# Ordering the prologue loads, warming the matmul clock, and loading the exp table one stage earlier in a macaron FFN + chunked-attention block

## The chip, the cores and the metric

The kernel runs on the 8 cores of one Trainium2 chip. Each core takes one batch row of 4096 frames, all cores read the same weights, and there is no traffic between cores. The metric is the device time of the slowest core in microseconds (us), median of several executions.

In most executions all cores agree within half a per cent and the records show a mean granted TensorE clock of 0.991 to 0.998. In some executions the cores of one die (cores 0 to 3, or 4 to 7) show a lower clock, down to 0.81, and the time is some per cent longer, up to 3430 us.

## The reference

```python
def reference(x, norm_ffn1, ffn1_w_gate, ..., norm_final):      # cut: the list of weights
    x = x + 0.5 * swiglu(rmsnorm(x, norm_ffn1), ffn1_w_gate, ffn1_w_up, ffn1_w_down)
    h = rmsnorm(x, norm_mix)
    z = h @ w_in                                   # q, k, v (512 each), u and vs (512 each), 2 x 1024 gate logits
    y_att = chunked_rel_attention(q, k, v, rel_bias)     # own 64-frame chunk and 8 chunks to the left
    y_sgu = gelu(u) * spatial_mix(layernorm(gelu(vs)))   # gMLP gating on 128-frame blocks
    x = x + (sigmoid(g_att) * (y_att @ w_branch_att) + sigmoid(g_sgu) * (y_sgu @ w_branch_sgu)) @ w_out
    x = x + 0.5 * swiglu(rmsnorm(x, norm_ffn2), ffn2_w_gate, ffn2_w_up, ffn2_w_down)
    return rmsnorm(x, norm_final)
```

x is (8, 4096, 1024) in float32, the FFN width is 2816, and there are 8 heads of 64.

## The kernel before

The sequence is cut into 8 tiles of 512 frames. The Python program records operations for five engines, and each engine then executes its own list strictly in order, waiting on semaphores where the recorder found a dependency. So the place at which an operation is recorded decides what stands in front of it. The stages run in this order:

- FFN 1 of tile 0, the first four pieces of FFN 1 of tile 1 ("ahead"), and the input projection of tile 0;
- then for each tile t: attention(t) interleaved with FFN 1 of tile t+1, the merge and output projection of t, the input projection of t+1, and FFN 2 of t. Attention 7 is interleaved with FFN 2 of tile 6.

`interleave` spreads the 144 steps of an attention evenly over the 60 pieces of an FFN (44 gate and up pieces of 8 matmuls, 16 down pieces of 11):

```python
def interleave(main, side, n_main, n_side):
    done = 0
    for i in range(n_main):
        next(main, None)
        want = (i + 1) * n_side // n_main
        while done < want:
            next(side, None)
            done += 1
    # cut: drain both
```

Weights stream through six SBUF buffers (`SLOT`, 1 MiB of bf16 each). At first a weight chunk is float32 in HBM: a casting DMA, issued on GpSimd, reads 2 MiB and writes 1 MiB. At a chunk's first, second or third use (spread over the chunks by `convert_use`) SP writes it back to HBM as bf16, and later uses read that copy.

```python
            def pump():
                while nxt[0] < len(chunk_order) and (nxt[0] < NSLOT or rel_flag.get(nxt[0] - NSLOT)):
                    # cut: which chunk, which buffer
                    if chunk not in converted:
                        p.dma("pool", ..., reads=[("X", 0, 3, 0)] if k == 1 else [], writes=[("slot", i)], sem=f"slotq{i}")
                    else:
                        p.dma("sp", ..., reads=[("SCR", chunk)], writes=[("slot", i)], sem=f"slot{i}")
```

The beginning: x of tile 0 on two queues, all six slots at once (slot 1 and its followers in GpSimd's list wait for x), then four RMS norms. A norm squares on ScalarE with a row sum, takes the reciprocal root on GpSimd (`add`, then `pow` with -0.5), scales on VectorE or ScalarE, and transposes on TensorE.

```python
            load_x(0)
            if not dry:
                pump()
            # cut
            for s in range(4):
                norm_sq(0, 0, s)
                if s:
                    norm_cp(0, 0, s - 1, "dve")
                    norm_tr(0, 0, s - 1)
            norm_cp(0, 0, 3, "dve")
            norm_tr(0, 0, 3)
```

Hooks put other work between the pieces of an FFN. In the first FFN these are the loads of x of tile 1 (piece 10), of the constants (piece 16), and seven memsets and a multiply on VectorE (piece 40). In later ones the last final-norm multiply of two tiles before goes to piece 0, in front of the first attention steps:

```python
                if t == 0:
                    add_hook(hk, 16, const_loads)
                    add_hook(hk, 50, const_loads_late)
                    add_hook(hk, 40, const_ops)
                    # cut: if n_tiles > 1
                        add_hook(hk, 10, P(load_x, 1))
                # cut
                    if t >= 2:
                        add_hook(hk, 0, P(final_mul, t - 2, 3))
```

(Calls of the projection are put on shared lines here.) The gating layernorm (`sgu_ln`) of a tile is recorded on VectorE and GpSimd inside the projection, behind the copies of q; v is copied out of PSUM by VectorE:

```python
                def post_u(cc, b):
                    p.add("act", ... func=AF.Gelu_apprx_tanh ...)
                def post_v(s, b):
                    p.add("dve", lambda e: e.tensor_copy(out=VR[:, half * 4 + s, :], in_=bank(b)), ...)
                def post_q(cc, b):
                    # cut: two scaled copies on ScalarE
                    sgu_ln(cc)
                # cut
                win_rows(t, 4, post_vs); win_cols(t, 3, post_u); win_rows(t, 2, post_v)
                win_cols(t, 0, post_q);  win_cols(t, 1, post_k)
```

An attention step records the scores of item i, the normalisation of i-2, the transposes of i-3 and the product with v of i-4. Scores are summed with the bias and reduced on VectorE (`SC`, `ASTAT`), exponentiated on ScalarE (`PB`), transposed on TensorE and copied out of PSUM by ScalarE (`PTS`). There is one PSUM area for scores and one for transposes, so the scores of item i+1 wait until VectorE has read those of item i.

## Time and profile before

| | before |
|---|---|
| median of 3 runs | 2905.71 us (2902.48 to 2908.49) |
| span of the profiled execution, slowest core (6) | 2902.5 us |
| span, mean of 8 cores | 2897.5 us |
| mean granted clock, all cores | 0.994 to 0.996 |
| TensorE busy | 2799.8 us |

The page of the profile gives, for each engine, its busy time, share and instructions; then the span in 40 slices with the busy share in tenths:

```profile
PE 2799.8 (96%) x15372; PEld 1375.4 (47%) x15680; DVE 1262.0 (43%) x2468; ACT 1002.9 (35%) x1772; POOL 181.6 (6%) x420
...
PE   4999999999999999999999999999999999999998
```

TensorE (PE) is the bound. A full group of 8 matmuls starts every 1.73 us in this trace, and nothing in the change touches the number of matmuls of the model. Only the roughly 100 us in which TensorE is idle or slow can be won. The list of waits says where they are. Its columns are the waiting line, what it waited for, then us in total, number of waits, and the longest. L444 is a transpose of a norm, L482, L500 and L526 are the gate, up and down matmuls of an FFN, L683 and L687 are scores:

```profile
PE ps L444 <- DVE XN L431: 35.2, 4, 28.8
PE ps L683 <- DVE ASTAT L692: 14.6, 8, 2.1
PE ps L687 <- DVE ASTAT L692: 5.0, 1, 5.0
PE ps L526 <- DVE HT L509: 3.5, 2, 3.3
...
PE ps L482 <- DMA SLOT<-fsrc: 3.0, 1, 3.0
```

So: 35 us before the first matmuls; about 2.1 us at the start of each of attentions 1 to 6; 5.0 us in attention 0; 3.3 us behind the memsets at 125 us; 3.0 us for a weight slot.

The start, in order of time (columns: start, duration, engine and line, operation, output and input, shape and count, and in brackets the idle time before it and what ended it):

```profile
28.79 1.01 PE L444 MATMUL ps<-IDB,XN 128*128 128x128 bf16 x8 [28.79 <-DVE XN L431]
...
40.73 3.37 PE L482 MATMUL ps<-XT,SLOT 128*128 128x512 bf16 x8 [1.48 <-DVE XT L448]
43.94 1.89 PE L500 MATMUL ps<-XT,SLOT 128*128 128x512 bf16 x8
```

The first full group takes 3.37 us and later ones 1.89 us: the first runs at about half clock. (This is read from the durations; the clock records of this core begin at 43.8 us, with the full clock.)

The DMA engines are not idle meanwhile. This is their strip for the first 140 us on core 1, 40 slices of 3.5 us, busy share in tenths and GB/s written:

```profile
DMA  2999999999999999999999999999999999997100
GB/s 63 239 221 233 231 247 365 246 216 166 178 181 166 145 157 160 164 174 178 167 165 180 178 146 161 176 180 173 167 176 174 171 174 178 166 175 144 28 0 0
```

They are full from 3.5 us to about 126 us. A weight stream alone writes 160 to 180 GB/s, which means reading twice as much.

The start of attention 1, on all engines. The second scores are issued at 563.24 us (not shown), and the third have to wait:

```profile
561.13 1.28 DVE L827 SCALAR_TENSOR_TENSOR X<-X,STAT,GF 128x1024 f32<-128x1024 f32 x1
...
562.33 0.75 DVE L692 CUSTOM_DVE_ANT_0 SC<-ps,RB 128x576 f32<-128x576 f32 x1
...
563.17 1.28 ACT L699 ACT_TABLE_LOAD   x1 [2.81 <-DVE ASTAT L692]
...
564.46 0.78 ACT L699 ACTIVATE PB<-SC,ASTAT 128x576 bf16<-128x576 f32 x1
...
565.98 0.69 DVE L490 SCALAR_TENSOR_TENSOR TG<-TG,ps 128x512 f32<-128x512 f32 x1 [2.29 <-ACT TG L488]
...
567.49 0.32 PE L683 MATMUL ps<-KT,QBD 128*128 128x384 bf16 x1 [2.13 <-DVE ASTAT L692]
```

Read it backwards. The third scores wait for VectorE's reduction of the second (L692, at 566.59 us). That stands behind L490, which waited for ScalarE's tanh (L488), which stood behind the first exp (L699), which stood behind the load of the exp table: 1.28 us. The final-norm multiply (L827, 1.28 us) stands in front of the first reduction.

### The profile page before, as it was taken

Reading aid. Unit: us, or ns where it says so; the run is one execution under the profiler, and the core shown is the slowest. Engines: PE = TensorE matmul, PEld = TensorE weight load, DVE = VectorE, ACT = ScalarE, POOL = GpSimd, SP = SyncE. Lnnn points to the kernel's source line nnn. Section 1 sums busy time; section 2 is a strip of 40 time slices with the busy share of each in tenths; the row PEclk is TensorE's granted clock in tenths of the full one; section 3 lists DMA queues with packets and bytes.
Section 4 is the critical chain, followed back from the end, with each engine's and each line's share of the span. In section 5 each row is a group of like instructions: output and inputs, shape, how many; then the busy total and the mean of one; then the engine's idle time right before and its main releaser. Section 6 shows DMA issues by size and latency. Waiting matters only on the chain.

```text
span 2902.5 us, 44394 instructions; the slowest of 8 cores (2892.6 to 2902.5 us)
## 1 busy us (share of the span) xinstructions
PE 2799.8 (96%) x15372; PEld 1375.4 (47%) x15680; DVE 1262.0 (43%) x2468; ACT 1002.9 (35%) x1772; POOL 181.6 (6%) x420
## 2 busy tenths in 40 slices
PE   4999999999999999999999999999999999999998
PEld 2444444455444554445544454444544445445444
DVE  1336443364424644246442464425544255466332
ACT  1223332253322533224332343324433244345221
POOL 1110111100100000000000000000000000000000
PEclk9999999999999999999999999999999999999999
DMA  9899899997897434543444534445344452432352
GB/s 192 138 206 187 171 226 174 212 243 203 225 213 253 168 127 158 180 160 139 145 148 164 174 124 162 144 152 200 123 150 169 157 189 99 158 129 102 139 188 95
DMA packets 103434, 485.39 MB, mean 167 GB/s; under 512 B 8880, under 2 KB 9520, under 8 KB 85936
## 3 DMA queue, kind: packets, MB, share of 16 engines
q1 hardware_dynamic: 82288, 387.49, 38.4%
q0 software_dynamic: 20352, 93.92, 20.0%
q8 instruction: 131, 2.15, 0.3%
q10 hardware_dynamic: 576, 1.13, 0.1%
q14 instruction: 87, 0.71, 0.1%
HBM read 511.40 MB, written 65.01 MB: 199 GB/s over the span
## 4 chain that ended last, share of the span: by engine, by line
PE 85%; DVE 4%; DMA 4%; issue 4%; ACT 1%; POOL 1%; SPq 0%; DVEq 0%; ACTq 0%; POOLq 0%
PE ps L526 21%; PE ps L482 18%; PE ps L500 17%; PE ps L764 8%; PE ps L549 4%; PE ps L775 4%; PE ps L796 3%; PE ps L563 3%; PE ps L719 2%; DMA ffs<-SLOT 2%; PE ps L731 2%; PE ps L444 1%; DVE SC L692 1%; PE ps L687 1%; DMA wis<-SLOT 1%
## 5 line engine op out<-in xcount | busy, mean ns | idle before, releaser
L482 PE MATMUL ps<-XT,SLOT 128*128 128x512 bf16 x2718 | 664.4, 383 | 12.0 <-DMA SLOT<-fsrc 3.0
L500 PE MATMUL ps<-XT,SLOT 128*128 128x512 bf16 x2766 | 663.0, 380 | 2.7
L526 PE MATMUL ps<-SLOT,HT 128*128 128x512 bf16 x2738 | 623.6, 380 | 8.9 <-DVE HT L509 3.5
L509 DVE TENSOR_TENSOR HT<-ps,TG 128x512 bf16<-128x512 f32 x350 | 240.9, 689 | 431.4 <-PE ps L500 295.0
L482 PEld LDWEIGHTS ps<-XT,SLOT 128*128 128x128 bf16 x2816 | 270.4, 98 | 310.1 <-issue 16.2
L526 PEld LDWEIGHTS ps<-SLOT,HT 128*128 128x128 bf16 x2816 | 270.8, 98 | 307.1 <-issue 8.2
L500 PEld LDWEIGHTS ps<-XT,SLOT 128*128 128x128 bf16 x2816 | 269.5, 98 | 300.7 <-issue 4.7
L699 ACT ACTIVATE PB<-SC,ASTAT 128x576 bf16<-128x576 f32 (+7 forms) x256 | 190.7, 745 | 455.0 <-DVE ASTAT L707 358.2
L494 ACT ACTIVATE TG<-ps 128x512 f32<-128x512 f32 x178 | 106.1, 597 | 448.7 <-PE ps L482 423.3
L532 DVE SCALAR_TENSOR_TENSOR X<-ps,X 128x512 f32<-128x512 f32 x128 | 88.6, 692 | 383.3 <-PE ps L526 372.6
L764 PE MATMUL ps<-XT,SLOT 128*128 128x512 bf16 x999 | 238.1, 379 | 1.3
L490 DVE SCALAR_TENSOR_TENSOR TG<-TG,ps 128x512 f32<-128x512 f32 x174 | 119.7, 688 | 246.6 <-ACT TG L488 240.3
L692 DVE CUSTOM_DVE_ANT_0 SC<-ps,RB 128x576 f32<-128x576 f32 (+7 forms) x256 | 182.6, 713 | 43.7 <-PE ps L687 42.1
L722 ACT ACTIVATE PTS<-ps 128x640 bf16<-128x640 bf16 (+4 forms) x256 | 167.7, 655 | 39.7 <-PE ps L719 39.6
L549 PE MATMUL ps<-XT,SLOT 128*128 128x512 bf16 x751 | 167.5, 379 | 0.9
L769 ACT ACTIVATE TG<-ps,BG 128x512 f32<-128x512 f32 x128 | 87.9, 686 | 231.4 <-PE ps L764 231.4
L779 DVE SCALAR_TENSOR_TENSOR TG<-TG,ps 128x512 f32<-128x512 f32 x128 | 88.0, 688 | 175.5 <-PE ps L775 160.7
L448 DVE TENSOR_TENSOR XT<-ps,G 128x1024 bf16<-128x1024 bf16 x96 | 115.7, 1218 | 96.2 <-PE ps L444 96.2
L764 PEld LDWEIGHTS ps<-XT,SLOT 128*128 128x128 bf16 x1024 | 98.7, 98 | 112.3
L383 POOL TENSOR_SCALAR STAT<-STAT 128x1 f32<-128x1 f32 x128 | 24.5, 191 | 1923.9 <-ACT XN L417 1599.0
L417 ACT ACTIVATE XN<-X 128x1024 bf16<-128x1024 f32 x72 | 76.0, 1056 | 192.9 <-DVE X L801 80.2
L816 ACT ACTIVATE XN<-X 128x1024 bf16<-128x1024 f32 x32 | 33.8, 1057 | 251.3 <-DVE X L532 251.3
(78 smaller groups left out, 2363.2 us busy)
## 6 DMA issues: line engine op xcount, KB each, us to landing
SLOT<-ffs SPq DMA_DIRECT2D x128, 1024.0 KB, 5.8
SLOT<-fsrc POOLq DMA_DIRECT2D x48, 1024.0 KB, 17.7
SLOT<-wds SPq DMA_DIRECT2D x47, 1024.0 KB, 5.0
SLOT<-mgs SPq DMA_DIRECT2D x52, 768.0 KB, 5.4
SLOT<-wis SPq DMA_DIRECT2D x35, 1024.0 KB, 5.2
ffs<-SLOT SPq DMA_DIRECT2D x22, 1024.0 KB, 17.0
SLOT<-wds SPq DMA_DIRECT2D x23, 768.0 KB, 4.2
SLOT<-wd POOLq DMA_DIRECT2D x17, 1024.0 KB, 16.7
```

The lines of the kernel that those rows point to most:

```text
L448: p.add("dve", lambda e: e.tensor_tensor(out=XT[xt][:, :, s * 128:(s + 1) * 128], in0=pbf.rearrange("p (k c) -> p k c", k=8), in1=gb, op=A ...
L482: p.add("pe", lambda e, kc=kc, W=W, bg=bg: e.matmul(bank(bg), lhsT=W[:, kc * 128:(kc + 1) * 128], rhs=xt[:, kc, :], start=(kc == 0), stop= ...
L490: p.add("dve", lambda e, buf=buf, bg=bg: e.scalar_tensor_tensor(out=buf[:], in0=buf[:], scalar=1.0, in1=bank(bg), op0=ALU.add, op1=ALU.mul ...
L500: p.add("pe", lambda e, kc=kc, W=W, bu=bu: e.matmul(bank(bu), lhsT=W[:, 1024 + kc * 128:1024 + (kc + 1) * 128], rhs=xt[:, kc, :], start=(k ...
L509: p.add("dve", lambda e, buf=buf, bu=bu, fc=fc: e.tensor_tensor(out=HT[:, fc, :], in0=bank(bu), in1=buf[:], op=ALU.mult), reads=[rb(bu), b ...
L526: p.add("pe", lambda e, fc=fc, W=W, by=by, s=s: e.matmul(bank(by), lhsT=HT[:, fc, s * 128:(s + 1) * 128], rhs=W, start=(fc == 0), stop=(fc ...
L549: p.add("pe", lambda e, kc=kc, W=W, b=b, cc=cc: e.matmul(bank(b), lhsT=W[:, kc * 512 + cc * 128:kc * 512 + (cc + 1) * 128], rhs=XT[t % 2][ ...
L692: p.add("dve", lambda e: e.tensor_tensor_reduce(out=sc[:, 0:nb], in0=S2[:, 512 - n_prev * 64:512 + n_cur * 64], in1=RB[:, hp, j0:576], sca ...
L699: p.add("act", lambda e: e.activation(out=pbuf[:, off + j0:off + 576], in_=sc[:, 0:nb], func=AF.Exp, bias=ASTAT[:, a0:a0 + 1], scale=-1.0, ...
L722: p.add("act", lambda e: e.activation(out=PTS[i % 2][:, kt0 * 128:640], in_=pt[:, kt0 * 128:640], func=AF.Copy), reads=[rb(6)], writes=[(" ...
L764: p.add("pe", lambda e, kc=kc, W=W, bgt=bgt, j=j: e.matmul(bank(bgt), lhsT=W[:, j * 1024 + kc * 128:j * 1024 + (kc + 1) * 128], rhs=XT[par ...
L775: p.add("pe", lambda e, c4=c4, W=W, bbr=bbr, j=j, Y=Y: e.matmul(bank(bbr), lhsT=W[:, 2048 + j * 512 + c4 * 128:2048 + j * 512 + (c4 + 1) * ...
```

## The change

The intent, part by part:

- **Gated loads.** x of tile 1 now waits for block `HT` 7 of the FFN's hidden layer and the constants for `HT` 16, so x of tile 0 and the first weights have the DMA engines to themselves. The FFN computes its blocks in the order 6, 7, 16, 17, ..., so these are its second and third blocks. Only slot 0 is issued before the norms' GpSimd work; the other five follow it.
- **Warm clock.** 24 dummy matmuls run while x is on its way. The norm's scalings alternate between VectorE and ScalarE.
- **Constant operations** are split over pieces 36, 18, 20 and 22.
- **First gating norm sooner.** For tile 0 `sgu_ln` moves from behind q to behind u.
- **Exp table ahead.** An Exp of one element per partition is recorded near the end of the FFN 2 that precedes an attention.
- **Attention paced by weights.** A down piece of the FFN counts 1.6, the others 1.0.
- The last **final multiply** of an earlier tile moves from piece 0 to piece 4.

```diff
-def interleave(main, side, n_main, n_side):
+def interleave(main, side, weights, n_side):
...
-        want = (i + 1) * n_side // n_main
+        past += w
+        want = int(past * n_side / total + 1e-6)
...
-                              reads=[("X", 0, 3, 0)] if k == 1 else [], writes=[("slot", i)], sem=f"slotq{i}")
+                              writes=[("slot", i)], sem=f"slotq{i}")
...
-                pump()
+                pump(1)
...
+            p.add("dve", lambda e: e.memset(XT[1][:, 0, :], 0.0), writes=[("XT", 1, 0)])
+            for _ in range(N_WARM):
+                p.add("pe", lambda e: e.matmul(bank(0), lhsT=XT[1][:, 0, 0:128], rhs=XT[1][:, 0, :], start=True, stop=True), ...)
...
-                p.dma("sp", lambda e: e.dma_start(out=BG[:], in_=bgate_d), writes=["BG"], sem="c2")
+                p.dma("sp", lambda e: e.dma_start(out=BG[:], in_=bgate_d), reads=[("HT", 16)], writes=["BG"], sem="c2")
...
-            N_FFN = 2 * NFC + 16
+            PACE = [1.0] * (2 * NFC) + [1.6] * 16
...  in post_u:
+                    if t == 0:
+                        sgu_ln(cc)
...  in post_q:
-                    sgu_ln(cc)
+                    if t:
+                        sgu_ln(cc)
...
+            def exp_table():
+                p.add("act", lambda e: e.activation(out=STAT[:, 40:41], in_=NHALF[:], func=AF.Exp),
+                      reads=["NHALF"], writes=[("st", 40)])
...
-                    add_hook(hk, 40, const_ops)
+                    for n in range(4):
+                        add_hook(hk, (36, 18, 20, 22)[n], P(const_ops, n))
...
-                        add_hook(hk, 10, P(load_x, 1))
+                        add_hook(hk, 6, P(load_x, 1, [("HT", 7)]))
...
-                        add_hook(hk, 0, P(final_mul, t - 2, 3))
+                        add_hook(hk, 4, P(final_mul, t - 2, 3))
...
+                if t + 2 < n_tiles:
+                    add_hook(hk, down(1, 3) - 1, exp_table)
...
             for s in range(4):
                 norm_sq(0, 0, s)
+            if not dry:
+                pump()
+            norm_cp(0, 0, 0, "dve")
+            for s in range(4):
+                if s < 3:
+                    norm_cp(0, 0, s + 1, "dve" if s % 2 else "act")
+                norm_tr(0, 0, s)
```

More of the change, by code (lines that the diff above doesn't have):

```diff
@@ L140, in __getattr__ @@
         return lambda *a, **k: None
-def interleave(main, side, n_main, n_side):
-    done = 0
-    for i in range(n_main):
+def interleave(main, side, weights, n_side):
+    total = sum(weights)
+    done = past = 0
+    for w in weights:
         next(main, None)
-        want = (i + 1) * n_side // n_main
+        past += w
+        want = int(past * n_side / total + 1e-6)
         while done < want:
@@ L239, in build_nc @@
         chunk_order = []
+        N_WARM = 24
         def run(p, dry):
@@ L280, in convert_use, with pump @@
                 return 0 if n % 4 == 0 else 1
-            def pump():
-                while nxt[0] < len(chunk_order) and (nxt[0] < NSLOT or rel_flag.get(nxt[0] - NSLOT)):
+            def pump(upto=1 << 30):
+                while nxt[0] < upto and nxt[0] < len(chunk_order) and (nxt[0] < NSLOT or rel_flag.get(nxt[0] - NSLOT)):
                     k = nxt[0]
@@ L322, in free_slot, with load_x @@
                     pump()
-            def load_x(t):
+            def load_x(t, after=()):
                 par = t % 2
@@ L331, in load_x @@
                           lambda e, par=par, s=s, r0=r0: e.dma_start(out=X[par][:, s, :], in_=x_d[r0:r0 + 128, :]),
-                          writes=[("X", par, s, 0), ("X", par, s, 1)], sem=f"x{par}{s}")
+                          reads=after, writes=[("X", par, s, 0), ("X", par, s, 1)], sem=f"x{par}{s}")
             p.dma("act", lambda e: e.dma_start(out=TG[0][:, 0:128], in_=ident_d), writes=[("TG", 0)], sem="c7")
@@ L337, in run @@
             if not dry:
-                pump()
+                pump(1)
             p.add("dve", lambda e: e.memset(NHALF[:], -0.5), writes=["NHALF"])
+            p.add("dve", lambda e: e.memset(XT[1][:, 0, :], 0.0), writes=[("XT", 1, 0)])
+            for _ in range(N_WARM):
+                p.add("pe", lambda e: e.matmul(bank(0), lhsT=XT[1][:, 0, 0:128], rhs=XT[1][:, 0, :], start=True, stop=True),
+                      reads=[("XT", 1, 0)], writes=[rb(0)])
             p.add("dve", lambda e: e.tensor_copy(out=IDB[:], in_=TG[0][:, 0:128]), reads=[("TG", 0)], writes=["IDB"])
@@ L352, in const_loads, with const_ops @@
                 p.dma("pool", lambda e: e.dma_start(out=WST[:], in_=wst_d), writes=["WST"], sem="c8")
-            def const_ops():
-                p.add("dve", lambda e: e.memset(WST[:].rearrange("p (g i) -> p g i", g=8)[64:128, :, 0:64], 0.0),
-                      reads=["WST"], writes=["WST"])
-                p.add("dve", lambda e: e.tensor_scalar(out=BG[:], in0=BG[:], scalar1=0.5, scalar2=None, op0=ALU.mult),
-                      reads=["BG"], writes=["BG"])
-                p.add("dve", lambda e: e.memset(QBD[:].rearrange("p a b c -> p (a b c)"), 0.0),
-                      writes=[("QBD", i) for i in range(4)])
-                p.add("dve", lambda e: e.memset(VR[:].rearrange("p a b -> p (a b)"), 0.0),
-                      writes=[("VR", i) for i in range(8)])
-                for a in range(2):
-                    for b in range(2):
-                        p.add("dve", lambda e, a=a, b=b: e.memset(PB[a][b][:], 0.0), writes=[("PB", a, b)])
+            def const_ops(n):
+                if n == 0:
+                    p.add("dve", lambda e: e.memset(WST[:].rearrange("p (g i) -> p g i", g=8)[64:128, :, 0:64], 0.0),
+                          reads=["WST"], writes=["WST"])
+                    p.add("dve", lambda e: e.tensor_scalar(out=BG[:], in0=BG[:], scalar1=0.5, scalar2=None, op0=ALU.mult),
+                          reads=["BG"], writes=["BG"])
+                elif n == 1:
+                    p.add("dve", lambda e: e.memset(QBD[:].rearrange("p a b c -> p (a b c)"), 0.0),
+                          writes=[("QBD", i) for i in range(4)])
+                elif n == 2:
+                    p.add("dve", lambda e: e.memset(VR[:].rearrange("p a b -> p (a b)"), 0.0),
+                          writes=[("VR", i) for i in range(8)])
+                else:
+                    for a in range(2):
+                        for b in range(2):
+                            p.add("dve", lambda e, a=a, b=b: e.memset(PB[a][b][:], 0.0), writes=[("PB", a, b)])
             dn = [0]
@@ L453, in xt_all @@
                 return [("XT", t % 2, s) for s in range(4)]
-            N_FFN = 2 * NFC + 16
+            PACE = [1.0] * (2 * NFC) + [1.6] * 16
             N_EARLY = 4
+            N_HELD = 8
             def ffn(t, i, use_tanh, hooks=None, n_silu=0):
@@ L909, in run @@
                 norm_sq(0, 0, s)
-                if s:
-                    norm_cp(0, 0, s - 1, "dve")
-                    norm_tr(0, 0, s - 1)
-            norm_cp(0, 0, 3, "dve")
-            norm_tr(0, 0, 3)
+            if not dry:
[5 more added lines that the diff above has]
+                norm_tr(0, 0, s)
             h0 = ffn1_hooks(0)
@@ L939, in run @@
                     if t == 0:
-                        interleave(ahead, attention(t), N_FFN - N_EARLY, N_ATT)
+                        interleave(ahead, attention(t), PACE[N_EARLY:], N_ATT)
                     else:
-                        interleave(ffn(t + 1, 0, True, ffn1_hooks(t + 1)), attention(t), N_FFN, N_ATT)
+                        interleave(ffn(t + 1, 0, True, ffn1_hooks(t + 1)), attention(t), PACE, N_ATT)
                     add_hook(mh, 0, P(norm_cp, t + 1, 1, 3))
@@ L966, in run @@
                     else:
-                        add_hook(hk, D1 + 8, P(norm_tr, t + 1, 2, 2))
-                        hk[D1 + 9] = chain(P(norm_tr, t + 1, 2, 3), hk[D1 + 9])
+                        add_hook(hk, D1 + N_HELD, P(norm_tr, t + 1, 2, 2))
+                        hk[D1 + N_HELD + 1] = chain(P(norm_tr, t + 1, 2, 3), hk[D1 + N_HELD + 1])
                         rest = ffn(t, 1, True, hk)
-                        interleave(itertools.islice(rest, D1 + 8), attention(t + 1), D1 + 8, N_ATT)
+                        interleave(itertools.islice(rest, D1 + N_HELD), attention(t + 1), PACE[:D1 + N_HELD], N_ATT)
                 else:
```

## The prediction

> **What bounds it now.** TensorE: the page has it busy 2799.8 of 2902.5 us, and the groups of instructions show full pace (8 matmuls of 128x512 in 1.73 us). So at most about 100 us can be won. By the list of waits and the timeline these are: 40.7 us before the first FFN matmul; 3.3 us at 125 us behind VectorE memsets; 3.0 us at 209.8 us for a weight slot; 5.0 us at 220 us for VectorE, held up by the gating layernorm; about 2.8 us more in attention 0; 2.12 us at the start of each of attentions 1 to 6; about 6.5 us in attention 7; 7.5 us at the end. Three of the 2.12 us gaps (924, 1634, 2344 us) are followed by a group at half clock, 3.4 instead of 1.8 us: the clock records drop to 0.5 for 3.41 us. The Trainium skill ("TensorE: Matmul & The Clock Gate", Part 1) says an idle window of about 3.4 us halves the clock; this trace agrees.
>
> **Prologue.** Before, x lands at 22.6 us because the next tile's x and the constants share the DMA engines, and GpSimd's first rsqrt waits for five weight issues (26.8 us). Gated, I estimate x at 15 us, first FFN matmul at 21 us, not 40.7. The 24 warming matmuls cost nothing, but I expect TensorE to cool while it waits for x, so the first group stays near 3.4 us. Most of the 20 us will not survive: the DMA share is 1.04 from 41 to 118 us, one weight slot lands every 6.1 us (2 MiB of source in 5.9 us is 355 GB/s; the skill, "DMA: Bandwidth & Descriptors", Specifications, gives 358 per core), and slots landed only 10 us ahead of use. The deferred loads (3.3 MB) now fall into that stream, and the DMA idles some 4 us between x and the second slot. TensorE will wait for weight slots (SLOT<-fsrc, SLOT<-wd) from about the third on. Gain at the end of the first FFN: 8 us (4 to 12), memset stall included.
>
> **Gating layernorm sooner (tile 0).** GpSimd's rsqrts pass two weight issues, so the layernorm starts about 17 us sooner, and the 5 us stall and its cold group go. But the four V copies now stand behind four layernorms (4.19 us each, waiting for GpSimd) on VectorE, so I expect a new TensorE wait for V's PSUM of some 5 to 8 us inside the projection. Net gain 3 us.
>
> **Attentions 1 to 6.** The exp table load (1.28 us) and the final multiply (1.28 us on VectorE) both lie in front of what the third score matmul waits for. With both gone, and attention thinned from 2.4 to 2.07 steps per up piece, the 2.12 us gaps and the three cold groups (1.65 us each) go: 12.7+5.0, less 2.7 for new small waits where the multiply and the denser down phase now sit: 15 us.
>
> **Attentions 0 and 7.** 1.5 us and 2.5 us: up pieces carry 8% fewer steps in attention 7; its table load stays.
>
> **Sum.** 8+3+15+1.5+2.5 = 30 us: **2876 us**, range 2862 to 2891. Faster by over 2% (below 2847.6): 0.03; within 2%: 0.96; slower: 0.01.
>
> **Right if:** first FFN matmul near 21 us; weight-slot waits totalling over 5 us before 120 us; end of the first FFN only 4 to 12 us earlier; no 2.1 us gaps on SC/ASTAT in attentions 1 to 6 and no table load there; a VR or L604 wait at 180 to 200 us.
>
> **Wrong if:** the weight stream runs faster once x and the constants no longer mix with it (then up to 20 us from the prologue, near 2862); the later DMA-bound stretch (up to 330 us) takes the gain back (near 2885); the final multiply or the down phase makes new stalls in every tile.

## The result, and the profile after

| | before | after |
|---|---|---|
| median, same rounds | 2907.1 us (2902.48 to 2911.58, 4 runs) | 2887.6 us (2885.88 to 2890.15, 4 runs) |
| ratio of fast runs | | 0.9934 (95%: 0.9916 to 0.9952) |
| profiled span, mean of 8 cores | 2897.5 us | 2881.1 us |
| profiled span, slowest core | 2902.5 us (core 6) | 2888.6 us (core 5) |

A ratio is the mean time of one kernel's fast runs over the mean of the other's in the same rounds, so it is not quite the ratio of the medians quoted beside it. Executions in which one die ran at a lower clock are left out of the means. The change is a small gain: 19.5 us by the medians, 16.4 us by the mean spans of the two profiled executions. The second number is the one that can be taken apart by stage.

```profile
PE 2820.3 (98%) x15704; PEld 1377.6 (48%) x15704; DVE 1263.8 (44%) x2467; ACT 1004.3 (35%) x1780; POOL 180.0 (6%) x420
...
PE   7889999999999999999999999999999999999998
```

TensorE is busy 20 us more, of which 7.4 us are the warming matmuls; some records of matmuls were missing in the trace before (15372 counted, 15704 now), so this line is no measure of the gain. The stages are. Each number below is the time of the first matmul of a stage, mean over the 8 cores, in us. The end of the first FFN is the first matmul of the FFN pieces "ahead"; a merge is counted from its first matmul on the attention's output, 1.7 to 1.8 us after its first gate matmul. An attention's length runs from its stage's first FFN matmul to its merge:

| stage begins | before | after | after minus before | gained or lost in the stage |
|---|---|---|---|---|
| first FFN matmul | 40.4 | 26.2 | -14.2 | |
| end of the first FFN | 164.6 | 161.4 | -3.2 | -3.2 from the start |
| attention 0 | 208.4 | 212.7 | +4.3 | +7.5 |
| merge of tile 0 | 341.9 | 340.9 | -1.0 | -5.3 |
| attentions 1 to 6, sum of their lengths | 873.0 | 858.7 | | -14.3 |
| attention 7, length | 133.4 | 131.2 | | -2.2 |
| span | 2897.5 | 2881.1 | -16.4 | |

The sum is -3.2 + 7.5 - 5.3 - 14.3 - 2.2 = -17.5. The missing +1 is TensorE waiting for a hidden-layer buffer (TG) in FFN 2 of tiles 0 and 1, where it grew, on the slowest cores, from 1.4 to 2.7 and from 2.2 to 3.6 us. There GpSimd's reciprocal roots stand behind weight issues.

The waits of the slowest core after the change (L456 transpose of a norm, L496 and L540 gate and down matmuls, L563 projection, L736 transposes in attention):

```profile
PE ps L456 <- ACT XN L441: 10.0, 1, 10.0
PE ps L563 <- DVE VR L604: 9.5, 1, 9.5
PE ps L736 <- ACT PTS L739: 9.3, 12, 1.2
PE ps L496 <- DMA SLOT<-fsrc: 9.1, 4, 4.2
PE ps L496 <- ACT TG L508: 3.6, 1, 3.6
PE ps L540 <- DMA SLOT<-wd: 3.0, 2, 2.4
```

Every row but the first is new or larger. The old ones (28.8 us at the start, 14.6 us on ASTAT, 5.0 us, 3.3 us of memsets) are gone or down to 2.0 us (ASTAT).

**The start.**

```profile
1.92 7.39 PE L346 MATMUL ps<-XT 128*128 128x512 bf16 x24 [1.92 <-DVE XT L344]
9.73 0.61 PE L456 MATMUL ps<-IDB,XN 128*128 128x128 bf16 x8 [0.42 <-DVE XN L443]
20.30 1.87 PE L456 MATMUL ps<-IDB,XN 128*128 128x128 bf16 x16 [9.96 <-ACT XN L441]
...
25.28 3.57 PE L496 MATMUL ps<-XT,SLOT 128*128 128x512 bf16 x8 [1.48 <-DVE XT L460]
```

The first FFN group starts 15 us sooner than before, still at half clock: 3.57 us. The warming ended at 9.3 us; after eight transposes of the first part of x, TensorE waited 10 us for the rest. The DMA strip of core 1 shows what the gates did:

```profile
DMA  2999800999999999999999999999999999999994
GB/s 53 263 195 195 204 11 6 149 135 143 157 178 239 234 214 217 226 181 182 205 123 196 238 245 173 165 151 184 179 173 171 169 183 165 178 174 169 166 174 64
```

From 17.5 to 24.5 us, two slices, the DMA engines move 11 and 6 GB/s: a hole. x of tile 0 is in, slot 0 is in, the next loads are held by the gates, and slots 1 to 5 are only issued once GpSimd has done its reciprocal roots. Later, from about 40 us on, rates of 205 to 245 GB/s appear between those of 160 to 180: there the postponed x and constants mix with the weights. TensorE, in a stretch where it had waited for no weights before, now waits 12.1 us in six waits between 70 and 124 us.

**The projection.**

```profile
181.35 0.72 POOL L300 DMA_DIRECT2D SLOT<-fsrc  x1 [8.84 <-DMA wis<-SLOT]
182.15 0.18 POOL L395 TENSOR_SCALAR STAT<-BNS 128x1 f32<-128x1 f32 x1
...
183.15 0.55 DVE L616 TENSOR_SCALAR HT<-HT,BNS,STAT 128x512 f32<-128x512 f32 x1 [10.01 <-POOL STAT L397]
...
197.75 2.48 DVE L604 CAST VR<-ps 128x512 bf16<-128x512 f32 x4
...
198.58 17.10 PE L563 MATMUL ps<-XT,SLOT 128*128 128x512 bf16 x64 [9.50 <-DVE VR L604]
```

GpSimd waits 8.84 us to issue a weight load whose slot is still being written back. Behind it stands the layernorm's reciprocal root; behind that, on VectorE, the rest of four layernorms; behind those, the four copies of v out of PSUM, which TensorE waits for. The wait is 4.0 us on three cores and 7.4 to 9.5 us on the other five, 6.6 us in the mean. It costs more than its length: on core 5 the granted clock is 0.5 for 10.24 us from 193.8 us on, and the 64 matmuls after the wait take 17.10 us, where eight groups of 1.73 us would be 13.8.

**Attention 1.**

```profile
554.04 1.28 ACT L768 ACT_TABLE_LOAD   x1
...
560.94 0.78 ACT L716 ACTIVATE PB<-SC,ASTAT 128x576 bf16<-128x576 f32 x1 [1.63 <-DVE ASTAT L709]
...
565.63 0.33 PE L700 MATMUL ps<-KT,QBD 128*128 128x384 bf16 x1
```

The table is loaded in the shadow of the last down matmuls; the third scores carry no wait. On cores 0 to 3 before, three to five groups per core at the starts of these attentions ran at half clock or partly so (2.7 to 3.5 us); after, there are none. But near the end of each of these attentions something new appears:

```profile
691.74 1.06 ACT L429 ACTIVATE XN<-X 128x1024 bf16<-128x1024 f32 x1 [2.69 <-DVE X L546]
...
692.79 1.13 ACT L441 ACTIVATE XN<-X,STAT 128x1024 bf16<-128x1024 f32 x1
693.83 0.68 ACT L739 ACTIVATE PTS<-ps 128x640 bf16<-128x640 bf16 x1
...
694.66 0.44 PE L736 MATMUL ps<-IDB,PB 128*128 128x128 bf16 x5 [0.88 <-ACT PTS L739]
```

ScalarE squares and scales for the next norm, and the copy that frees the transposes' PSUM stands behind: 0.88 us.

### The profile page after: what moved, and what is told of

The parts are those of the page before. It is cut to its first block, busy times and chain, and to the rows that moved or that the text cites. A ratio compares the mean times of both kernels' runs of the same rounds, so it can differ in the third digit from the quotient of the medians.

```text
span 2888.6 us, 44775 instructions; the slowest of 8 cores (2875.1 to 2888.6 us)
## 1 busy us (share of the span) xinstructions
PE 2820.3 (98%) x15704; PEld 1377.6 (48%) x15704; DVE 1263.8 (44%) x2467; ACT 1004.3 (35%) x1780; POOL 180.0 (6%) x420
## 3 DMA queue, kind: packets, MB, share of 16 engines
q10 hardware_dynamic: 576, 1.13, 0.1%
## 4 chain that ended last, share of the span: by engine, by line
PE 89%; DMA 6%; DVE 2%; issue 2%; ACT 1%; POOL 0%; ACTq 0%; DVEq 0%; POOLq 0%; SPq 0%
PE ps L540 20%; PE ps L496 19%; PE ps L514 19%; PE ps L785 8%; PE ps L563 5%; PE ps L796 4%; PE ps L817 3%; PE ps L577 3%; PE ps L736 2%; PE ps L748 2%; PE ps L456 1%; DMA ffs<-SLOT 1%; DMA SLOT<-fsrc 1%; DMA SLOT<-wd 1%; PE ps L704 1%
## 5 line engine op out<-in xcount | busy, mean ns | idle before, releaser
L496 PE MATMUL ps<-XT,SLOT 128*128 128x512 bf16 x2816 | 671.2, 381 | 14.1 <-DMA SLOT<-fsrc 9.1
L514 PE MATMUL ps<-XT,SLOT 128*128 128x512 bf16 x2816 | 667.1, 380 | 0.0
L540 PE MATMUL ps<-SLOT,HT 128*128 128x512 bf16 x2816 | 634.2, 379 | 5.7 <-DMA SLOT<-wd 3.0
L496 PEld LDWEIGHTS ps<-XT,SLOT 128*128 128x128 bf16 x2816 | 271.7, 98 | 323.2 <-issue 24.5
L540 PEld LDWEIGHTS ps<-SLOT,HT 128*128 128x128 bf16 x2816 | 269.9, 98 | 305.6 <-issue 7.1
L514 PEld LDWEIGHTS ps<-XT,SLOT 128*128 128x128 bf16 x2816 | 269.4, 98 | 297.2 <-issue 4.9
L785 PE MATMUL ps<-XT,SLOT 128*128 128x512 bf16 x1024 | 241.9, 379 | 0.0
L709 DVE CUSTOM_DVE_ANT_0 SC<-ps,RB 128x576 f32<-128x576 f32 (+7 forms) x256 | 182.8, 714 | 43.7 <-PE ps L704 21.8
L563 PE MATMUL ps<-XT,SLOT 128*128 128x512 bf16 x768 | 171.5, 384 | 9.5 <-DVE VR L604 9.5
L785 PEld LDWEIGHTS ps<-XT,SLOT 128*128 128x128 bf16 x1024 | 98.7, 98 | 112.3
L429 ACT ACTIVATE XN<-X 128x1024 bf16<-128x1024 f32 x72 | 76.0, 1056 | 188.5 <-DVE X L546 93.6
L563 PEld LDWEIGHTS ps<-XT,SLOT 128*128 128x128 bf16 x768 | 75.5, 99 | 101.0 <-issue 14.6
```

The source lines that it names most:

```text
L496: p.add("pe", lambda e, kc=kc, W=W, bg=bg: e.matmul(bank(bg), lhsT=W[:, kc * 128:(kc + 1) * 128], rhs=xt[:, kc, :], start=(kc == 0), stop= ...
L514: p.add("pe", lambda e, kc=kc, W=W, bu=bu: e.matmul(bank(bu), lhsT=W[:, 1024 + kc * 128:1024 + (kc + 1) * 128], rhs=xt[:, kc, :], start=(k ...
L540: p.add("pe", lambda e, fc=fc, W=W, by=by, s=s: e.matmul(bank(by), lhsT=HT[:, fc, s * 128:(s + 1) * 128], rhs=W, start=(fc == 0), stop=(fc ...
L563: p.add("pe", lambda e, kc=kc, W=W, b=b, cc=cc: e.matmul(bank(b), lhsT=W[:, kc * 512 + cc * 128:kc * 512 + (cc + 1) * 128], rhs=XT[t % 2][ ...
L709: p.add("dve", lambda e: e.tensor_tensor_reduce(out=sc[:, 0:nb], in0=S2[:, 512 - n_prev * 64:512 + n_cur * 64], in1=RB[:, hp, j0:576], sca ...
L785: p.add("pe", lambda e, kc=kc, W=W, bgt=bgt, j=j: e.matmul(bank(bgt), lhsT=W[:, j * 1024 + kc * 128:j * 1024 + (kc + 1) * 128], rhs=XT[par ...
```

## The experiments

All results were correct. Runs that share a chip and its runs of the kernel before are named together: e1, e2, e4 and e9 (kernel before: median 2907.43 us of 7, fast ones 2901.54 to 2907.43); e5 to e8 (one run, slow, 3204.82 us); e3, e10 and f1 (2908.76 us of 11); g1 (2908.71 us of 11). Stage times, means of 8 cores of the profiled execution, us:

| | first FFN matmul | end of first FFN | attention 0 | merge of tile 0 | span |
|---|---|---|---|---|---|
| before | 40.4 | 164.6 | 208.4 | 341.9 | 2897.5 |
| after | 26.2 | 161.4 | 212.7 | 340.9 | 2881.1 |
| e1, layernorm late | 25.7 | 161.5 | 205.2 | 337.8 | 2876.5 |
| e2, no gates | 30.2 | 152.5 | 203.1 | 331.2 | 2870.8 |
| e3, no warming | 26.3 | 164.2 | 216.3 | 344.3 | 2885.2 |
| e4, v copied by ScalarE | 25.7 | 161.0 | 204.1 | 334.8 | 2873.0 |
| e9, prologue alone | 25.9 | 162.0 | 206.1 | 340.6 | 2896.3 |
| e10, gates, all slots at once | 26.9 | 157.5 | 208.4 | 336.6 | 2876.5 |
| f1, no gates and v by ScalarE | 30.6 | 155.0 | 199.4 | 333.4 | 2871.4 |
| g1, no gates, weight 1.3, multiply back | 30.5 | 155.3 | 206.5 | 333.8 | 2879.3 |

A warning on this table: e2, f1 and g1 have the same code up to the end of the first FFN and reached it at 152.5, 155.0 and 155.3 us on three chips. Differences of 3 us between runs of different chips are not resolved there. Each row is one profiled execution.

Theory at the start: the prologue lost most of its 14 us to the gates (hole and mixing), and the early layernorm costs more than it saves. Rivals: the weight stream is simply too slow whatever the order; the DMA-bound stretch up to 330 us takes any gain back anyway.

### e1_ln_late: after, with the layernorm of tile 0 behind q again

```diff
-                    if t == 0:
-                        sgu_ln(cc)                 # in post_u
...
-                    if t:
-                        sgu_ln(cc)                 # in post_q
+                    sgu_ln(cc)
```

> The changed kernel with one part undone: tile 0's gating layernorm goes back behind the q projection. Stage times are the first matmul of a stage, mean of the eight cores. Theory (the move turned the 5 us wait at the first scores into a longer wait for V's PSUM): no TensorE wait on the V copies (4.0 to 9.5 us in the changed kernel); the wait on SC/ASTAT at the first scores of attention 0 is back with 1 to 6 us; first FFN ends at 161.4 as in the changed kernel; merge of tile 0 starts 1 to 4 us sooner than the changed kernel's 340.9, and the whole is 0 to 3 us faster than it. Rival (the move helped, and the loss is elsewhere): merge of tile 0 starts 3 to 6 us later than 340.9.

Measured: one fast run, 2884.62 us; the other three slow. The stages of the fast run: the projection is 7.5 us shorter (43.7 us from the end of the first FFN to attention 0, against 51.3), the wait for v is gone, and in attention 0 waits for scores and weight slots come back (132.6 us, against 128.2). The merge begins 3.1 us sooner. So moving the layernorm up, which I had put at a gain of 3 us, cost about 3 us.

### e2_ungated: after, without the two gates

```diff
-                p.dma("sp", ... in_=bgate_d), reads=[("HT", 16)], writes=["BG"], sem="c2")
+                p.dma("sp", ... in_=bgate_d), writes=["BG"], sem="c2")
...
-                        add_hook(hk, 6, P(load_x, 1, [("HT", 7)]))
+                        add_hook(hk, 6, P(load_x, 1))
```

> The changed kernel with the gates on the next tile's x and on the constants taken away, all else kept. Theory (the first FFN is bound by the weight stream, so the time TensorE starts does not count): first FFN matmul 4 to 8 us later than 26.2, yet the first FFN ends within 2 us of 161.4, or up to 3 us sooner as the hole in the DMA between x and the second slot is filled; TensorE waits less for slots (under 6 us instead of 12). Rival (the early start is worth something): the end of the first FFN moves later by about as much as the start, 165 or more.

Measured: fast runs 2877.63, 2874.31 and 2875.54 us (a fourth was slow), ratio to the kernel before 0.9903 (0.9884 to 0.9923). The first FFN matmul comes 4 us later than with gates, and the first FFN ends 8.9 us sooner, which is more than I had allowed. The DMA strip of core 1 has no hole:

```profile
DMA  3999999999999999999999999999999999999299
GB/s 72 287 255 227 240 249 312 242 146 156 164 162 178 174 167 166 180 167 170 179 170 165 174 171 141 181 168 179 169 178 167 168 166 173 180 162 165 39 142 166
```

The deferred x and constants are loaded in the first 28 us (227 to 312 GB/s), when TensorE has nothing to do anyway, and from then on the weight stream runs alone. Of the waits for weights little is left on core 1:

```profile
PE ps L563 <- DVE VR L604: 4.0, 1, 4.0
PE ps L540 <- DMA SLOT<-wd: 3.6, 2, 2.2
```

With gates the same core had 7.7 + 4.3 us of them. The gain lasts: the merge begins 9.7 us sooner, and the mean span is 10.3 us shorter.

### e10_slots_at_once: after, gates kept, all six slots issued first

```diff
-                pump(1)
+                pump()
```

> The changed kernel, gates kept, but all six weight slots issued at once at the start instead of one before and five after the first rsqrts. It fills the hole in the DMA between 10 and 30 us with weights instead of with the deferred loads. Theory (the hole is what the gates cost): first FFN matmul later than 26.2, 30 to 42 us, as x shares with the weights, yet the first FFN ends 5 to 10 us sooner than 161.4 (151.5 to 156.5). Rival (the deferred loads hurt because they run slowly when mixed into the weight stream, wherever the hole is): the first FFN ends at 160 or later.

This fills the hole with weights and leaves the deferral, so it separates the two costs of the gates.

```profile
DMA  2999999999999999999999999999999999999689
GB/s 60 224 191 200 211 180 176 170 153 170 166 164 211 220 220 226 195 199 174 175 223 237 202 142 146 176 169 186 162 164 176 167 173 180 166 164 170 125 140 227
```

The hole is gone (180 and 176 GB/s). Measured: 2884.61, 2882.26, 2883.49 and 2884.59 us, ratio 0.9914 (0.9894 to 0.9934). The first FFN ends at 157.5 us. My theory had said 151.5 to 156.5, the rival 160 or later, and the result lies between. I had also expected a delayed start; it was not delayed (26.9 us).

To split the cost of the gates, runs of one chip have to be compared, since chips differ by about 3 us here. On the chip of e10 there are e3, with hole and deferral (164.2 us, though without warming), and f1, with neither (155.0 us). So of 9.2 us about 6.7 are the hole and about 2.5 the deferred loads. The whole agrees with the other chip: 161.0 to 162.0 us in e1, e4 and e9 against 152.5 in e2. The hole's 6.7 us is also its length, two slices of 3.5 us. (Comparing e10 with after and e2 across chips would give 3.9 and 5 us, the wrong order.) The split rests on one execution of each.

In the profile after, on core 1, slots 2 to 8 landed 7.0 to 9.8 us apart while the deferred loads were mixed in, 8.3 us in the mean, against about 6.1 us for a slot alone. That is 13.4 us over six slots. By volume alone the 3.3 MB would take about 9.6 us at 344 GB/s (an estimate: 2 MiB in 6.1 us), so most of it is the bytes themselves.

### e9_only_prologue: the prologue of the change alone

Layernorm, pace, multiply and exp table are as before:

```diff
-            PACE = [1.0] * (2 * NFC) + [1.6] * 16
+            PACE = [1.0] * (2 * NFC + 16)
...  (sgu_ln back in post_q for every tile)
-                        add_hook(hk, 4, P(final_mul, t - 2, 3))
+                        add_hook(hk, 0, P(final_mul, t - 2, 3))
...
-                    add_hook(hk, down(1, 3) - 1, exp_table)
+                    pass
```

> The prologue part alone (gated loads, warming matmuls, order of the first norms, memsets spread out); layernorm, pacing, exp table and final multiply as before. Theory: first FFN matmul at 26 us, first FFN ends 3 us sooner than before's 164.6 (161 to 162.5), merge of tile 0 starts 2 to 5 us sooner than before's 341.9, whole gain 2 to 5 us. Rival (the prologue is worth its 14 us, and the layernorm's move lost the rest): merge of tile 0 at 332 or sooner, whole gain 9 us or more.

Measured: median 2901.81 us of 4 fast runs, ratio 0.9996 (0.9978 to 1.0013). A matmul 14.5 us sooner at the start is 2.6 us at the end of the first FFN and 1.2 us at the merge of tile 0. That is less than even my theory had allowed (2 to 5 us at the merge). As it was built, the prologue is worth nothing that the total shows.

### e3_nowarm: after, no warming matmuls

```diff
-        N_WARM = 24
+        N_WARM = 0
```

> The changed kernel without the 24 warming matmuls, one look. Theory (TensorE cools again in the 10 us that it waits for the last part of x, and the first FFN is bound by the weight stream anyway): the first FFN group of 8 stays at 3.4 to 3.6 us; the first FFN ends within 1.5 us of 161.4 (mean of the eight cores, or of the undisturbed die). Rival (warming pays): the first transposes and groups are slower and the end of the first FFN moves 2 us or more later.

Measured, one look: 2894.95 us. The first FFN matmul starts at 26.3 us, as with warming, and its group takes 3.30 us, against 3.57 us with warming. The granted clock of the stretch of 20 to 30 us is 0.50 in the profile after. The warming held for the first eight transposes (0.61 us, against 1.01 without it) and was lost in the wait for x; more than that cannot be seen. The first FFN ends 2.8 us later than after, the rival's sign; but different chips show as much for the same code; whether the warming has any effect on the total stays open.

### e4_v_on_act: after, the v copies of tile 0 on ScalarE

```diff
                 def post_v(s, b):
+                    if t == 0:
+                        p.add("act", lambda e: e.activation(out=VR[:, half * 4 + s, :], in_=bank(b), func=AF.Copy), ...)
```

> The changed kernel with tile 0's four V copies moved from VectorE to ScalarE, so that they do not stand behind the layernorms. Theory (the VectorE queue alone made the wait): the 4.0 to 9.5 us wait on the V copies is gone and no wait of over 1 us takes its place before the attention; attention 0 starts at 205 to 207 instead of 212.7; merge of tile 0 starts 4 to 8 us sooner than 340.9 and the whole is 4 to 8 us faster than the changed kernel. Rival (this stretch is bound by the weight stream whatever TensorE does): new waits on SLOT<-fsrc take its place, and merge of tile 0 starts within 1.5 us of 340.9.

If the early layernorm hurts only because v stands behind it on VectorE, another engine for these four copies should keep its gain and drop its cost. Measured: 2881.86, 2881.71, 2880.64 and 2878.15 us, ratio 0.992 (0.9903 to 0.9937). The wait for v is gone, the projection is back to 43.1 us, attention 0 takes 130.7 us, and the merge begins 6.1 us sooner than after. That shows the mechanism of the lost projection time. Another 2.2 us of its shorter span come from attentions 1 to 6 (142.7 us each instead of 143.1, a gap of about 0.2 us at a transpose is missing). f1, on another chip, has the same 142.7 us and e2 does not, so it comes with this edit; I have no explanation for it.

### f1_ungated_v_on_act: both repairs together

The edits of e2 and e4 in one kernel.

> The changed kernel without the gates and with tile 0's V copies on ScalarE: the two repairs together. If they are independent and the stream of weights leaves room: first FFN ends at 152.5, no wait on the V copies, attention 0 starts at 195 to 199 and merge of tile 0 at 325 to 328 (334.8 and 331.2 with one repair each); whole 31 to 36 us faster than before (ratio 0.9876 to 0.9893). If the weight stream binds up to the merge: new SLOT<-fsrc waits near 200 us, merge of tile 0 at 330 or later, ratio 0.990 or more.

Measured: fast runs 2879.5, 2883.96, 2875.88 and 2885.4 us (two were slow), ratio 0.9906 (0.9886 to 0.9926): no better than e2. Attention 0 begins 3.7 us sooner than in e2, but the merge 2.2 us later. Attention 0 now runs into the weights:

```profile
204.68 2.97 PE L496 MATMUL ps<-XT,SLOT 128*128 128x512 bf16 x8 [4.09 <-DMA SLOT<-fsrc]
...
294.49 2.72 PE L540 MATMUL ps<-SLOT,HT 128*128 128x512 bf16 x6 [3.69 <-DMA SLOT<-wd]
```

So the rival that the DMA-bound stretch takes gains back is true, but only from here on. Of the 9 us from the gates it took nothing; of the 6 us that the v copies gave in e4 it took nearly all: from the end of the first FFN to the merge f1 needs 178.4 us, e2 178.7 and e4 173.8.

### e5_only_exp, e6_only_pace, e7_only_mul, e8_exp_mul: the parts of attention 1 to 6

Each is the kernel before with one part, or two. All four ran on a chip on which cores 4 to 7 were slowed; cores 0 to 3 had clocks of 0.996 to 0.999, and the numbers of e5 to e8 are of these four alone, the gaps and waits of core 1. The columns before and after are means of eight cores, on other chips. The totals of e5 to e8 are not used.

```diff
+ e5: def exp_table(): ...  and  add_hook(hk, down(1, 3) - 1, exp_table)  if t + 2 < n_tiles
+ e6: interleave(..., PACE, ...)  with  PACE = [1.0] * 44 + [1.6] * 16
+ e7: add_hook(hk, 4, P(final_mul, t - 2, 3))      # was 0
+ e8: e5 and e7
```

> The kernel before with the exp table load in the FFN ahead, alone. Measured on the stretch from the first matmul of an attention stage to its merge, tiles 2 to 6, mean of the eight cores: before 145.4 us, changed kernel 143.1. Theory (table load and final multiply lie in one chain, each 1.28 us of the 2.12 us gap at the third scores): the gap shrinks to 0.8 us and the half-clock groups after it go; the stretch is 1.3 to 2.2 us shorter. Rival (pacing is what removes the gap): under 0.7 us.

> The kernel before with the pacing by weights alone. Theory: the third scores come one up piece (1.73 us) later, so the 2.12 us gap shrinks to 0.4 us or less, but the denser down phase brings a new wait of 0.9 us on the copies of the transposed probabilities (PTS), as in the changed kernel; the stretch of tiles 2 to 6 is 1.0 to 2.2 us shorter than 145.4. Attention 7 (first matmul of its FFN to the merge's first is 133.4 before, 131.3 changed) gets the whole 2 us from it; in attention 0 PTS waits of about 3 us appear. Rival (the PTS wait is due to something else): no PTS wait of 0.88 us here.

> The kernel before with the final multiply of the tile before moved from hook 0 to hook 4, alone. Theory: same as the exp table alone, gap from 2.12 to 0.8 us, stretch of tiles 2 to 6 1.3 to 2.2 us shorter; nothing in tiles 0, 1 and 7. Rival (VectorE has slack there and the table load alone counts): gap stays 2.1 us.

> The kernel before with exp table and final multiply, without pacing. Theory: gap and half-clock groups gone, and no PTS wait: the stretch of tiles 2 to 6 is 2.5 to 3.2 us shorter than 145.4, so shorter than in the changed kernel (143.1); attention 7 unchanged. Rival (pacing is needed for the gain): 143.3 or longer.

| | before | e5 exp | e6 pace | e7 multiply | e8 exp, multiply | after |
|---|---|---|---|---|---|---|
| attentions 2 to 6, mean length | 145.4 | 143.2 | 143.8 | 144.4 | 143.6 | 143.1 |
| gap at the third scores | 2.13 | 0.85 | 0.40 | 1.18 (once 1.46) | 0.40 | 0 |
| new waits for PTS, attentions 1 to 6 | none | none | 0.88 | 0.81, some + 0.2 to 0.4 | 0.81, some + 0.2 to 0.4 | 0.88 |
| attention 7 | 133.4 | 133.6 | 131.1 | 133.5 | 133.8 | 131.2 |
| attention 0 | 133.5 | 133.5 | 133.0 | 133.2 | 134.6 | 128.2 |

In e5 the gap at the third scores of an attention is shorter by exactly the length of the table load, 2.13 - 1.28 = 0.85 us (core 1, attention 3):

```profile
1265.93 0.32 PE L683 MATMUL ps<-KT,QBD 128*128 128x384 bf16 x1 [0.85 <-DVE ASTAT L692]
```

No group at these starts runs at half clock any more in any of the four, at gaps of 0.40 to 1.46 us. That is the rest of e5's 2.2 us. The exp table alone thus gives 2.2 of the 2.3 us that an attention gained. The multiply alone gives 1.0 us, less than the 1.3 to 2.2 us I had expected; and the two together give 1.8 us, where I had expected 2.5 to 3.2: worse than the table alone. The list of waits of e8 shows why not more came of it (twelve waits on core 1: 0.81 us in each of attentions 1 to 6, 0.2 to 0.4 us more in four of these, and one of 0.32 us in attention 7 that the kernel before has too):

```profile
PE ps L719 <- ACT PTS L722: 6.6, 12, 0.8
```

Moved four pieces back, the multiply and what it displaces meet the transposes: the gap at the scores shrinks, and 0.81 us, in some attentions 0.2 to 0.4 us more, open at the transposes. The pace alone gives 1.6 us, and all of the 2.2 us of attention 7, where nothing else of the change acts. The parts do not add up, because they remove the same gap.

### g1_ungated_pace13: e2 with a smaller weight, and the multiply back at piece 0

```diff
-            PACE = [1.0] * (2 * NFC) + [1.6] * 16
+            PACE = [1.0] * (2 * NFC) + [1.3] * 16
...
-                        add_hook(hk, 4, P(final_mul, t - 2, 3))
+                        add_hook(hk, 0, P(final_mul, t - 2, 3))
```

> A version put together from the experiments: the changed kernel without the gates, the final multiply back at hook 0 (the table load alone gave 143.2 of 143.1 us), and a weight of 1.3 instead of 1.6 for the down pieces, the least that still brings the third scores one up piece later. If the 0.88 us PTS wait per tile comes from the dense down phase: it is gone or under 0.4 us and the stretch of tiles 2 to 6 is 142.2 to 142.7 us instead of 143.1; first FFN ends at 152 to 155, merge of tile 0 at 330 to 333; whole 0.9875 to 0.9905 of before, a little under the 0.9903 of the ungated kernel. If the PTS wait has another cause: it stays, and the stretch is 143.1 or longer, as the gap at the third scores comes back (0.85 us).

Measured: fast runs 2885.64, 2886.82, 2892.51 and 2888.13 us (two were slow), ratio 0.9933 (0.9911 to 0.9954), a miss. Attentions 1 to 6 take 143.3 us, attention 7 133.9 us. The 0.88 us wait for PTS stayed, so a weight of 1.3 does not avoid it. That does not clear the denser down phase: e6 has the wait with the weight of 1.6 alone, and e5, with all weights equal, has none; a weight between 1.0 and 1.3 was not tried. In the trace the square and copy of the next norm stand in front of it on ScalarE (1.06 + 1.13 us, shown above); no run moved them. The gap of 0.40 us at the scores came back. The weight of 1.3 is no better than 1.6.

The best version measured is e2, the change without its gates: 2874.31 to 2877.63 us. The intervals of its ratio, and those of f1, e4, e10 and after, overlap, so this order rests on the stage times more than on the totals.

## Why the prediction was right or wrong

The range (2862 to 2891) held; the point, 2876 us, was 11.6 us too low. All the mechanisms named in it are in the trace. Two terms of the sum were too large, one of them with the wrong sign. That the range held in spite of this, by 3.4 us, it owes to its width of 29 us and to attentions 1 to 7, which came as predicted; for tile 0 it was luck.

- **Prologue, predicted 8 us (4 to 12); measured 3.2 us at the end of the first FFN, below the interval, and 1.2 us at the merge when the prologue stands alone (e9).** The signs foretold were there: half clock in the first group (3.57 us), waits for slots of 12.1 us. Mis-sized were the two costs of the gates. x landed at 17.9 us, not 15, and the first FFN matmul came at 25.3 us on the slowest core, not 21. The hole in the DMA, put at "some 4 us" in the prediction, was two slices of 3.5 us with nearly nothing moved. The 3.3 MB of deferred loads were named but not priced: they made a slot take 8.3 us in the mean instead of 6.1. e10, with the runs of its chip, puts the hole at about 6.7 us of the end of the FFN and the deferral at about 2.5 us; e2, with neither, ended the FFN 12.1 us before the kernel before, the upper edge of my interval.
- **Layernorm sooner and attention 0, predicted 3 + 1.5 = 4.5 us gained; measured 2.2 us lost between the end of the first FFN and the merge.** The step that failed is "net gain 3 us". The 5.0 us stall did go, and attention 0 became 5.3 us shorter. But the projection became 7.5 us longer. I had foreseen "5 to 8 us" for the wait for v; it was 4.0 to 9.5, and new waits for PTS in attention 0 (1.19, 1.00 and 0.94 us) come on top; e6 showed the same kind with the pace alone. e1 measures the move alone at 3.1 us lost by the merge. The wait was rightly sized and wrongly netted: a net gain of 3 us after a wait of 5 to 8 means that I had counted on 8 to 11 us saved, and e1 shows 4.4 us (attention 0 takes 132.6 us with the layernorm late, 128.2 with it early).
- **Attentions 1 to 6, predicted 15 us, measured 14.3 us.** Size and mechanism were right: the gaps, the table load and the groups at half clock went. The allowance of 2.7 us for new waits was half of what came, 0.88 us in each of six, 5.3 us; part of that was made good by more groups at half clock than I had counted (three on core 6, three to five on cores 0 to 3). And the credit was wrongly shared: I gave the multiply as much as the table load. e5 shows that the table load with the half-clock groups behind it does nearly all of it, and e8 that the multiply adds nothing to it.
- **Attention 7, predicted 2.5 us, measured 2.2 us.** e6 shows that the pace alone does it.
- **Not foreseen:** about 1 us of longer TG waits in FFN 2 of tiles 0 and 1.

Together: -30 predicted; -3.2 + 2.2 - 14.3 - 2.2 + 1 = -16.5, against -16.4 measured. Of the ways to be wrong that the prediction named, "the weight stream runs faster once x and the constants no longer mix with it" did not happen: the gates moved the mixing from a time when TensorE was idle to a time when it needed weights. "The later DMA-bound stretch takes the gain back" happened only in f1. "New stalls in every tile" happened, at 0.88 us each.

What stays open: the exact split between hole and mixing; the effect of the warming matmuls on the total; which part of the down phase makes the 0.88 us wait; and 2.2 us of e4.

## What to carry to other kernels

Where a weight stream bounds the beginning, an earlier first matmul can be worth nothing by itself (e9); ask when the last byte needed arrives, keep the DMA engines full from the first microsecond, and load other things while the compute engine is idle rather than holding them back into the stream. Before moving work forward on an in-order engine, list what stood there and who waits for it (the copies of v), and look for another engine for that. When several changes remove the same gap, try each alone: here one tiny Exp gave nearly all of what three changes gave.

## What the Trainium skill lacked or had wrong

- "TensorE: Matmul & The Clock Gate", Part 1: The HAM clock gate, says that the array is cold after an idle window of about 3.4 us and warm after about 3.4 us of activity. The clock records of the trace before, which drop to 0.5 for 3.41 us at a time, agree with the length of the window, and so does the failed warming (7.4 us of matmuls, then a wait of 10 us, then a first FFN group of 3.57 us at half clock). As a rule for how long a gap may be, the figure is too generous: single gaps of 2.1 us were followed by groups at half clock in some attentions of every core looked at (2.7 to 3.6 us instead of 1.89 us), while none of the gaps of 0.40 to 1.46 us at the same places was. The page (HAM oscillation) puts the abstract rule as no idle gaps above about 3.4 us; here a gap of 2.1 us was already too long.
- "ScalarE: Activation LUTs", What ACT_TABLE_LOAD costs, gives about 1283 ns for the load and about 1380 ns for a drain, 2.66 us a switch. The trace agrees on the load (1.28 us). Taking it off the chain at the start of an attention shortened the gap by 1.28 us (2.13 to 0.85), so no drain lay on this chain, where ScalarE had idled 2.81 us before the load.
- "DMA: Bandwidth & Descriptors", Specifications, gives about 358 GB/s of HBM bandwidth per core; the weight stream alone agrees (2 MiB read per 6.1 us is 344 GB/s). No page I read gives a rate for casting loads with plain loads beside them: a slot of 1 MiB written then took 7.0 to 9.8 us, 8.3 in the mean, instead of 6.1 us.
- No page I read warns that small arithmetic on GpSimd stands behind weight loads issued there: a reciprocal root of 0.7 us had to wait behind an issue that itself waited 8.84 us for its slot's write-back, and the chain behind it ended in TensorE's wait of 9.5 us for v.
